# One more plain hidden pair, layer-1 modulation products on TensorE, and later sums in a two-layer diffusion block

## The chip, the cores and the metric

The kernel runs on one core of a Trainium2 chip. Its time is the device time of one execution in microseconds (us), and the number compared is the median over several runs. The profile is one further execution, recorded by the hardware.

## The reference

Two token streams pass two layers: 512 latent tokens and 256 context tokens, each 1024 wide. Layer 0 mixes with a gated linear recurrence and layer 1 with latent attention. After each mixer stands a gated feed-forward network with 2816 hidden units. Every norm is modulated by six vectors per layer that come from a condition `c` (latent) or `c_ctx` (context). Cut to what matters here:

```python
for i in range(DEPTH):                       # DEPTH = 2
    mod_lat = split(silu(c)    @ ada_w[i] + ada_b[i], 6)   # ada_w[i]: 1024 x 6144
    mod_ctx = split(silu(c_ctx) @ ada_w[i] + ada_b[i], 6)
    h = modulate(rmsnorm(x, norm_mix_g[i]), mod[0], mod[1])
    x = x + mod[2] * mixer_i(h)
    h = modulate(rmsnorm(x, norm_ffn_g[i]), mod[3], mod[4])
    x = x + mod[5] * ((silu(h @ Wg) * (h @ Wu)) @ Wout)    # 2816 hidden units = 22 tiles of 128
return rmsnorm(x, final_norm_g)
```

In layer 1 the context stream is needed by the attention alone (modulation vectors 0 and 1). The vectors 2 to 5 of layer 1 are used for latent tokens only.

## The kernel before, in words

Every large product is made from split operands: a float32 value is cut into a high and a low part (`wh`/`wl` for weights, `hh`/`hl` for normed tokens, `ah`/`al` for hidden activations), and three matmuls (high x high, low x high, high x low) stand for one. Tokens lie along the free dimension: latent 0 to 511, context 512 to 767.

**Weights.** `Stream` brings weights in: SyncE's queue loads up to 1 MB into one of two `raw` buffers, ScalarE makes `wh` (L108), VectorE (GpSimd in some stages) makes `wl` (L119). Four pairs of `wh`/`wl` units exist. `done(unit)` gives units back in order and lets `advance` split the next ones at this place of ScalarE's and VectorE's programs. Each engine works its own list in program order, and the program order is written by hand.

**Layer 0's feed-forward network** is `ffn0`. The 22 hidden tiles come in chunks of `PAIRS0 = (4, 2, 4, 4, 4, 4)`. After the hidden tiles of a chunk come eight output tiles (`out_tile`, m = 0 to 7), each added into `xT` by `residual` (L760) with a multiply-add on VectorE for latent and one for context tokens.
A hidden tile is a pair of products, gate and up. The first `PLAIN0` pairs are `plain`: two products of 48 matmuls each into two-bank PSUM tiles (`ps_main`, three of them). The others are `pair`: the gate and up blocks for two halves of the 768 tokens (A = 0 to 383, B = 384 to 767) are taken as a 2 x 2 block product made of seven products of 12 matmuls (in the order 1, 5, 6, 2, 7, 3, 4) into three one-bank PSUM tiles x, y, z. For these, `differences(kp)`, called four times, makes sums and differences of token blocks on VectorE and ScalarE (48 VectorE operations in all), and `sums` / `sum4` (L365 to L372) do the like for each weight tile.
Between plain pairs and seven-product pairs the PSUM layout changes from three two-bank tiles to six one-bank tiles. An output tile takes two banks. `split_hidden` cuts a hidden tile into `ah` and `al`; for a seven-product pair it is put off into the next pair, or to the end of the chunk. The first two output tiles of a chunk are begun with all but the last hidden tile.

**Layer-1 modulation.** `ada_w[1]` comes in 96 tiles of 128 x 512 (GpSimd's queue, 256 KB each, three buffers): six vectors `ch`, two halves each, eight row blocks `k` each. A call of `ada_step` is a *place* in the program; it takes one tile or `n` tiles. Each tile costs VectorE a multiply-add into `acc` (`ada_sum`, L535/L537), and for `ch` 0 and 1, needed for both streams, a second one for the other stream (L540/L542). When the eight tiles of a half are summed, the next call makes `ada_add`: small fp32 matmuls with a column of ones (`pick`, L558) sum over the 128 partitions into the PSUM tile `psada`. After the second half `ada_copy` (ScalarE, L565) takes it out, and some calls later `ada_evac` transposes it on TensorE (L519) and adds the bias. Layer 0's vectors 2 to 5 were made during the recurrence by another way: fp32 matmuls with `csil` (silu of both conditions, 32 columns wide) as stationary and the weight tile as moving operand, four column groups of 256 columns (L584).
By the code, 80 tiles of layer 1 (`ch` 0 to 4) are taken during `ffn0`: one at each plain pair, one in each `pair` (after product 2), one or two after each output tile. `ada_until(1, 4)` takes what is left behind the last hidden tile, ahead of the last eight output tiles. By the order of the calls six tiles are left there. The last 16 tiles (`ch` 5) are taken in `ffn(1, ...)`, three calls after each of the first hidden tiles.

Of the kernel before, what the change touches and what calls it, by code (L numbers as in the profile page):

```python
# [145 lines left out]
def kernel(ctx, tc, x, c, ctx_in, c_ctx, ada_w, ada_b, norm_mix_g, norm_ffn_g, ffn_w_in,  # L146
# [194 lines left out]
    PLAIN0 = 3  # L341
# [166 lines left out]
    def ada_evac(wait=False):  # L508
# [11 lines left out]
        pv = px[:, :256].rearrange("p (c j r) -> p j c r", c=2, j=4)  # L520
        for v in range(2):
            dve.tensor_tensor(mod[:, l, ch, v, :].rearrange("p (j c) -> p j c", j=4), pv[:, :, :, v],
                              adab(l, ch).rearrange("p (j c) -> p j c", j=4), op=ALU.add)
# [6 lines left out]
    def ada_sum(i, t, l, ch, k, half):  # L530


        both, first = ch < 2, acc[:, :512]
        if k == 0:
            dve.tensor_scalar(first, t, csil[:, k, int(both):int(both) + 1], None, op0=ALU.mult)  # L535
        else:
            dve.scalar_tensor_tensor(first, t, csil[:, k, int(both):int(both) + 1], first, op0=ALU.mult, op1=ALU.add)  # L537
        if both:
            if k == 0:
                dve.tensor_scalar(t, t, csil[:, k, 0:1], None, op0=ALU.mult)  # L540
            else:
                dve.scalar_tensor_tensor(t, t, csil[:, k, 0:1], ada_ps["lat"], op0=ALU.mult, op1=ALU.add)  # L542
            ada_ps["lat"] = t
        if k == KT - 1:
            ada_state["sums"] = (i, l, ch, half, [t, first] if both else [first])

    def ada_add():
        if ada_state["sums"] is None:
            return
        i, l, ch, half, sums = ada_state["sums"]  # L550
# [4 lines left out]
        for j in range(2):  # L555
            r = 64 * half + 32 * j
            for v, a in enumerate(sums):
                pe.matmul(ps[r:r + 32, :256], pick[:, v, :], a[:, j * 256:(j + 1) * 256],  # L558
                          start=v == 0, stop=v == len(sums) - 1)
# [7 lines left out]

    def ada_step(n=1):
        for _ in range(n):
            ada_evac(n == 1)  # L570
            ada_add()
            i = ada_state["used"]
            if i >= N_ADA[0]:
                return
            ada_fill()
            l, ch, k, *half = adas[i]
            t = ada_tiles.pop(i)
            if half:
                ada_sum(i, t, l, ch, k, *half)
            else:  # L580
                if k == 0:
                    ada_ps[0] = psa.tile([P, 512], F32, name=f"psada{i}", tag="ada")
# [1154 lines left out]
```

## Time and profile before

| what | value |
|---|---|
| median of 3 runs | 1620.7 us (1619.24 to 1623.19) |
| the profiled execution: its time / its span | 1622.39 / 1620.6 us |
| TensorE (PE) busy | 1516.2 us (94%) |
| VectorE (DVE) / ScalarE (ACT) / GpSimd (POOL) busy | 980.1 (60%) / 679.8 (42%) / 282.0 us (17%) |
| mean granted TensorE clock | 0.968 of full speed |

Busy time is the union of an engine's instructions, matmuls overlap one another in it. The granted clock is 1.00 at 2.4 GHz and 0.50 at 1.2 GHz; the value of a stretch is a mean over these two levels. A releaser (`<-`) names the instruction for which the engine waited. The stages around the change are: `ffn0`'s entry and plain pairs up to 427 us, its chunks to 898 us, the end of `ffn0` to 946 us, the attention to about 1225 us, and layer 1's feed-forward network from there.

### The profile page before, as it was taken

What the parts mean: (1) busy time and instruction counts of PE and PEld (TensorE: products, weight loads), DVE (VectorE), ACT (ScalarE), POOL (GpSimd) and SP (SyncE); (2) the same over time, 40 slices, a digit from 0 to 9 for tenths busy, and PEclk for the clock granted to TensorE, in tenths of its full rate; (3) what the DMA queues carried; (4) which work ended last, traced back from release to release, by engine and by line L of the source; (5) the groups of instructions that cost most, each with busy time, mean ns of one, the idle gap of its engine ahead of it and who ended that gap; (6) DMA issues with size and microseconds to landing.
All of it is one profiled execution on the core that took longest, in us unless ns stands there. A gap on an engine that the chain in (4) does not pass through costs nothing.

```text
span 1620.6 us, 21238 instructions
## 1 busy us (share of the span) xinstructions
PE 1516.2 (94%) x8667; PEld 1330.2 (82%) x8667; DVE 980.1 (60%) x1474; ACT 679.8 (42%) x998; POOL 282.0 (17%) x261
## 2 busy tenths in 40 slices
PE   7999989899799999999999799999999889999998
PEld 5887877688688998989889687899998668888887
DVE  5676777777877867767676466666537434323334
ACT  5476575543413331413314243666644222222223
POOL 3233333350000000011010243111144100000002
PEclk8999999999899999999999899999999999999999
DMA  9334343311233233243342222110112323233222
GB/s 359 113 118 127 107 130 93 103 58 41 73 97 104 85 98 98 82 146 105 105 143 86 65 59 69 28 41 27 53 53 92 137 85 104 79 104 114 79 80 91
DMA packets 137073, 155.11 MB, mean 96 GB/s; under 512 B 6283, under 2 KB 114432, under 8 KB 136976
## 3 DMA queue, kind: packets, MB, share of 16 engines
q1 hardware_dynamic: 124352, 112.21, 21.6%
q0 software_dynamic: 12320, 41.02, 8.2%
q8 instruction: 68, 1.11, 0.3%
q10 hardware_dynamic: 304, 0.53, 0.1%
q14 instruction: 29, 0.24, 0.0%
HBM read 151.64 MB, written 2.10 MB: 95 GB/s over the span
## 4 chain that ended last, share of the span: by engine, by line
PE 63%; issue 15%; DVE 15%; ACT 4%; DMA 1%; POOL 1%; SPq 0%; DVEq 0%; POOLq 0%; ACTq 0%
PE f L784 14%; PE fo L784 7%; PE fo L1206 6%; PE x L1160 4%; PE lo L784 3%; PE s L1536 3%; PE ga L784 2%; PE wo L784 2%; PE o L1578 2%; PE z L1160 2%; PE p L784 2%; PE g L784 2%; DVE yc L892 1%; PE t L1554 1%; PE y L1160 1%
## 5 line engine op out<-in xcount | busy, mean ns | idle before, releaser
L108 ACT ACTIVATE wh<-raw 128x1024 fp32r<-128x1024 f32 (+3 forms) x250 | 209.6, 865 | 215.7 <-PE fo L1206 63.5
L119 POOL TENSOR_TENSOR wl<-raw,wh 128x1024 fp32r<-128x1024 f32 (+3 forms) x66 | 158.1, 2406 | 327.2 <-ACT wh L108 321.5
L119 DVE TENSOR_TENSOR wl<-raw,wh 128x1024 fp32r<-128x1024 f32 (+2 forms) x184 | 170.4, 938 | 11.9 <-ACT wh L108 11.8
L760 DVE SCALAR_TENSOR_TENSOR xT<-fo,mod,xT 128x512 f32<-128x512 f32 (+1 forms) x124 | 74.3, 626 | 129.3 <-PE fo L1206 65.7
L239 POOL DMA_DIRECT2D ada<-in_ada_w_dram x96 | 51.7, 539 | 559.3 <-DVE ada L542 280.8
L784 PE MATMUL f<-hh,wh 128*128 128x512 f32 x320 | 126.1, 394 | 0.0
L784 PE MATMUL f<-hl,wh 128*128 128x512 f32 x320 | 125.5, 392 | 0.0
L784 PE MATMUL f<-hh,wl 128*128 128x512 f32 x320 | 125.3, 392 | 0.0
L778 POOL TENSOR_TENSOR acc<-acc,sq 128x256 f32<-128x256 f32 (+1 forms) x52 | 50.6, 973 | 335.4 <-ACT sq L776 334.2
L1206 PE MATMUL fo<-ah,wh 128*128 128x512 f32 (+1 forms) x352 | 100.2, 352 | 1.6 <-ACT ah L1194 1.6
L1101 DVE TENSOR_TENSOR sg<-sg,f 128x512 f32<-128x512 f32 x20 | 13.8, 688 | 142.1 <-ACT sg L1100 142.1
L1206 PE MATMUL fo<-al,wh 128*128 128x512 f32 (+1 forms) x352 | 98.6, 347 | 0.6 <-DVE al L1195 0.6
L1206 PE MATMUL fo<-ah,wl 128*128 128x512 f32 (+1 forms) x352 | 98.0, 345 | 0.0
L1100 ACT ACTIVATE sg<-f 128x512 f32<-128x512 f32 x20 | 12.0, 599 | 163.8 <-PE f L784 163.8
L784 PE MATMUL fo<-ah,wh 128*128 128x512 f32 (+1 forms) x200 | 72.9, 364 | 0.0
L784 PE MATMUL fo<-ah,wl 128*128 128x512 f32 (+1 forms) x200 | 72.7, 364 | 0.0
L784 PE MATMUL fo<-al,wh 128*128 128x512 f32 (+1 forms) x200 | 72.7, 364 | 0.0
L784 PEld LDWEIGHTS f<-hh,wh 128*128 128x128 f32 x320 | 60.8, 190 | 14.1 <-issue 1.6
L784 PEld LDWEIGHTS f<-hh,wl 128*128 128x128 f32 x320 | 60.6, 189 | 12.8
L784 PEld LDWEIGHTS f<-hl,wh 128*128 128x128 f32 x320 | 60.8, 190 | 12.6
L1206 PEld LDWEIGHTS fo<-ah,wh 128*128 128x128 f32 x352 | 59.4, 198 | 11.9 <-issue 2.9
L537 DVE SCALAR_TENSOR_TENSOR acc<-ada,csil,acc 128x512 f32<-128x512 f32 x84 | 62.8, 747 | 6.5 <-DMA ada<-in_ada_w_dram 5.6
(480 smaller groups left out, 4073.6 us busy)
## 6 DMA issues: line engine op xcount, KB each, us to landing
raw<-in_ffn_w_in_dram SPq DMA_DIRECT2D x24, 1024.0 KB, 4.9
ada<-in_ada_w_dram POOLq DMA_DIRECT2D x96, 256.0 KB, 3.1
raw<-in_ffn_w_in_dram SPq DMA_DIRECT2D x40, 512.0 KB, 4.8
raw<-in_ffn_w_out_dram SPq DMA_DIRECT2D x19, 1024.0 KB, 5.0
ada<-in_ada_w_dram POOLq DMA_DIRECT2D x30, 512.0 KB, 4.4
ada<-in_ada_w_dram SPq DMA_DIRECT2D x32, 256.0 KB, 5.5
raw<-in_lru_w_in_dram SPq DMA_DIRECT2D x10, 512.0 KB, 5.1
raw<-in_lru_gate_w_dram SPq DMA_DIRECT2D x16, 256.0 KB, 3.1
```

Of the source, the lines that this page charges most:

```text
L108: nc.scalar.activation(dst(hi), src(self.raw[load]), AF.Copy)
L119: self.low_engine.tensor_tensor(dst(lo), src(self.raw[load]), dst(hi).bitcast(F32), op=ALU.subtract)
L239: eng.dma_start(t, ada_w[l, k * P:(k + 1) * P, c0:c0 + 512])
L537: dve.scalar_tensor_tensor(first, t, csil[:, k, int(both):int(both) + 1], first, op0=ALU.mult, op1=ALU.add)
L760: dve.scalar_tensor_tensor(xT[:, m, s], ps(s) if callable(ps) else ps[:, s], mod[:, l, ch, v, m:m + 1], xT[:, m, s], op0=ALU.mult, op1=ALU ...
L778: accs.append(lambda: nc.gpsimd.tensor_tensor(acc[:, s], acc[:, s], sq, op=ALU.add))
L784: pe.matmul(ps[:, off + s.start:off + s.stop], a, b[:, s], start=first and i == 0, stop=last and i == 2)
L892: dve.scalar_tensor_tensor(y[:, s0:s1], ps[:, s0 + o:s1 + o], convw(tap, k), y[:, s0:s1], op0=ALU.mult, op1=ALU.add)
L1160: pe.matmul(ps, w[:, o:o + P], x[:, k0 + k, s], start=first and k == 0 and q == 0, stop=last and k == 3 and q == 2, skip_group_check=not f ...
L1206: pe.matmul(ps[v], w[:, o:o + P], x[:, k, s], start=k == 0 and q == 0, stop=k == nh - 1 and q == 2)
L1536: pe.matmul(ps[:, o:o + 384], x, y[:, k0:k1], start=j == 0, stop=j == 4)
L1578: pe.matmul(ps[:, :256], x[:, t % 4, hs], y[:, t, :], start=t == 0 and j == 0, stop=t == NT - 1 and j == 2)
```

## The change

- `PLAIN0` goes from 3 to 4: the whole first chunk is plain, and the first seven-product pair is that of hidden tile 4. `differences(1)` and later ones use another pool of temporaries, and the four `differences` are spread among the plain pairs in another order. The splits of plain pairs 2 and 3 and the copies of the late difference block go behind the last plain pair.
- `ada_product`: for `ch` 0 and 1 of layer 1 the 32 tiles are no longer summed on VectorE. Each is the moving operand of four fp32 matmuls of 128 columns in four column groups, with `csil` as the stationary operand, accumulated in `psada` over `k`.
- `ada_step`: with a finished half waiting, the first call does nothing, and only the second makes `ada_add`.
- In `pair` a call stands after product 1, and while `ch` 0 and 1 last a second one after product 2. In `ffn(1, ...)` there are two tiles between the gate and the up product and two behind the pair, in place of three behind it. After output tiles: one tile each while `ch` 0 and 1 last or in chunk 1, two later.
- Three output tiles are begun early in place of two (in the first chunk with two of four hidden tiles). The banks of a pair are taken as y, z, x. The last pair of a chunk is split at once, ahead of the release of its last weight unit.

```diff
     PAIRS0 = (4, 2, 4, 4, 4, 4)
-    PLAIN0 = 3
+    PLAIN0 = 4
...
     def ada_sum(i, t, l, ch, k, half):
...
+    def ada_product(i, t, l, ch, k, half=None):
+        n = 256 if half is None else 128
+        if k == 0 and not half:
+            ada_ps[0] = psa.tile([P, 512], F32, name=f"psada{i}", tag="ada")
+        o = (half or 0) * n
+        for j in range(4):
+            pe.matmul(ada_ps[0][32 * j:32 * j + 32, o:o + n], csil[:, k, :], t[:, j * n:(j + 1) * n],
+                      start=k == 0, stop=k == KT - 1)
+        if k == KT - 1 and half != 0:
+            ada_copy(i, l, ch, ada_ps[0])
+    def ada_one():
+        ada_fill()
+        i = ada_state["used"]
+        l, ch, *f = adas[i]
+        (ada_sum if l and ch > 1 else ada_product)(i, ada_tiles.pop(i), l, ch, *f)
+        ada_state["used"] += 1
+        ada_fill()
     def ada_step(n=1):
+        if ada_state["sums"]:
+            ada_state["calls"] += 1
+            if ada_state["calls"] < 2:
+                return
+            ada_add()
+        else:
+            ada_evac(True)
         for _ in range(n):
-            ada_evac(n == 1)
-            ada_add()
...
-            ada_fill()
+            if ada_state["used"] < N_ADA[0] and not ada_state["sums"]:
+                ada_one()
...
                     if pg is None:
                         pg, pu, off = pair_ps(f"f{l}{ph}{j}")
                         prod(pg, gu, hh, hl, sl)
+                        ada_step(2)
                         prod(pu, uu, hh, hl, sl, off=off)
                     elif pu is None:
                         pu, off = pg, SEQ
...
                     dve.tensor_tensor(al[:, j, :n], sg[:, :n], ah[:, j, :n].bitcast(F32), op=ALU.subtract)
                     st.done(gu)
                     st.done(uu)
-                    ada_step()
-                    ada_step()
-                    ada_step()
+                    ada_step(2)
                 if ph == 0:
                     ada_until(1, 5)
                 lastp = ph == len(ffn_units[l]) - 1
...
             def differences(kp):
-                if kp == 1:
+                if kp:
                     x = [[stemp(f"x{kp}{i}")[:, :H2] for i in range(2)], [ptemp(f"x{kp}{i}") for i in (2, 3)]]
                 else:
                     x = [tmp.tile([P, T], F32, name=f"x{kp}{i}", tag="nt") for i in range(2)]
...
                     st.done(s0_out[c][2][m // per])
             split = []
-            LATONLY = lambda: ada_state["used"] > 8 * KT
-            def pair(j, i):
+            on_pe = lambda: ada_state["used"] < 8 * KT
+            def pair(j, i, last):
                 g = tmp.tile([P, T], F32, name=f"g0{j}", tag="nt")
                 p5 = ptemp(f"p5{j}")
-                x, y, z = (ps_bank(f"{c}{j}")[:, :H2] for c in "xyz")
+                y, z, x = (ps_bank(f"{c}{j}")[:, :H2] for c in "yzx")
                 product(1, j, x, True, True)
                 act.activation(g[:, A], x, AF.Copy)
                 while split:
                     split.pop()()
                 release(1, j)
+                ada_step()
                 product(5, j, z, True, True)
                 act.activation(p5, z, AF.Copy)
                 release(5, j)
...
                 dve.tensor_tensor(g[:, A], g[:, A], y, op=ALU.add)
                 act.activation(g[:, A], g[:, A], AF.Silu)
                 release(2, j)
-                ada_step()
+                if on_pe():
+                    ada_step()
                 product(7, j, x, False, True)
                 dve.tensor_tensor(p5, p5, x, op=ALU.add)
                 release(7, j)
...
                 product(4, j, x, False, True)
                 dve.tensor_tensor(g[:, B], g[:, B], p5, op=ALU.mult)
                 dve.tensor_tensor(g[:, A], g[:, A], x, op=ALU.mult)
-                split.append(lambda: split_hidden(i, g))
+                if last:
+                    split_hidden(i, g)
+                else:
+                    split.append(lambda: split_hidden(i, g))
                 release(4, j)
             def plain(j, pg, pu):
...
                 if pu is None:
                     pu = ps_main(f"f0{j}u")
                     prod(pu, uu, hh, hl, SL)
-                if j == PLAIN0 - 1:
-                    act.activation(th[3], late[0].bitcast(F32), AF.Copy)
-                    dve.tensor_copy(tl[3], late[1].bitcast(F32))
                 g = tmp.tile([P, T], F32, name=f"g0{j}", tag="nt")
                 act.activation(g, pg[:, :T], AF.Silu)
                 dve.tensor_tensor(g, g, pu[:, :T], op=ALU.mult)
-                split_hidden(j, g)
+                if j < 2:
+                    split_hidden(j, g)
+                else:
+                    split.append(lambda: split_hidden(j, g))
                 st.done(gu)
                 st.done(uu)
-                ada_step()
             made = [ps_main(f"f0{j}g") for j in range(2)] + [ps_main("f00u")]
             entry([(s0_plain[0][0], made[0], 0, True), (s0_plain[1][0], made[1], 0, True),
...
             st.low_engine = dve
             plain(0, made[0], made[2])
             differences(0)
+            plain(1, made[1], None)
+            ada_step()
             differences(1)
-            plain(1, made[1], None)
+            plain(2, None, None)
+            ada_step()
             differences(2)
             differences(3)
-            for j in range(2, PLAIN0):
-                plain(j, None, None)
+            plain(3, None, None)
+            act.activation(th[3], late[0].bitcast(F32), AF.Copy)
+            dve.tensor_copy(tl[3], late[1].bitcast(F32))
+            ada_step()
+            while split:
+                split.pop(0)()
             ps_layout((6, 512))
             for c, (h0, nh, outs) in enumerate(s0_out):
                 for j in range(max(h0, PLAIN0), h0 + nh):
-                    pair(j, j - h0)
+                    pair(j, j - h0, j == h0 + nh - 1)
                 lastp = c == len(s0_out) - 1
-                while split:
-                    split.pop()()
                 if lastp:
                     ada_until(1, 4)
                     for m in range(KT):
...
                     boundary([lambda m=m: last(m) for m in range(KT)], nxt, at=(1, 2, 1))
                     return
-                two = [out_tile(c, m, (gb, ga), range(nh - 1)) for m in range(2)]
+                n0 = nh - 1 if c else 2
+                three = [out_tile(c, m, (gb, ga), range(n0)) for m in range(3)]
                 for m in range(KT):
-                    ps = out_tile(c, m, (gb, ga), (nh - 1,) if m < 2 else range(nh), two[m] if m < 2 else None)
+                    if m < 3:
+                        ps = out_tile(c, m, (gb, ga), range(n0, nh), three[m])
+                    else:
+                        ps = out_tile(c, m, (gb, ga), range(nh))
                     for g in (gb, ga):
                         residual(m, lambda s: ps[g[0]], 0, 5, g, False)
                     out_done(c, m)
-                    ada_step(1 if nh == 4 and not LATONLY() else 2 if nh == 4 else m % 2)
+                    ada_step(1 if nh < 4 or on_pe() else 2)
     na1 = Norm(1, 1, 0, CTXG, hh, hl, "m1a")
     nb1 = Norm(1, 1, 0, LATG, hh, hl, "m1b")
```

## Rows read from the trace of the kernel before

**Rows 1.** TensorE's waits from 387.2 to 908.9 us: in total, times, longest.
```profile
PE psada L558 <- DVE acc L537: 13.8, 3, 9.2
PE x L1160 <- DVE g L1265: 7.4, 1, 7.4
PE psada L558 <- DVE ada L542: 5.5, 3, 3.7
PE adax L519 <- ACT acc L565: 4.0, 3, 2.8
PE x L1160 <- DVE p L1240: 3.7, 4, 0.9
PE f02u L784 <- ACT wh L108: 2.9, 1, 2.9
PE f02u L784 <- DVE wl L119: 2.2, 1, 2.2
```
**Rows 2.** Stretches: length, PE, PEld, DVE, ACT, POOL busy, clock, DMA share, GB/s.
```profile
387.20:444.30 57.10, 44.61 (x230) 40.02 (x229) 48.66 (x82) 23.93 (x39) 1.61 (x3) 0.88 0.22 70
444.30:480.60 36.30, 34.76 (x202) 29.75 (x201) 26.68 (x42) 5.70 (x10) 3.77 (x7) 1.00 0.35 102
480.60:533.70 53.10, 49.77 (x275) 45.57 (x274) 40.01 (x65) 16.75 (x30) 3.23 (x6) 0.97 0.31 95
533.70:635.30 101.60, 96.00 (x540) 89.64 (x539) 71.81 (x114) 32.52 (x57) 6.46 (x12) 0.97 0.30 91
635.30:737.70 102.40, 97.83 (x550) 90.32 (x549) 71.99 (x117) 34.08 (x60) 10.76 (x20) 0.97 0.38 114
737.70:838.10 100.40, 95.68 (x541) 89.30 (x540) 67.25 (x110) 31.83 (x56) 10.76 (x20) 0.98 0.37 115
838.10:897.60 59.50, 59.35 (x341) 58.13 (x339) 42.02 (x67) 26.92 (x49) 3.23 (x6) 1.00 0.34 107
897.60:908.90 11.30, 1.57 (x8) 0.62 (x7) 7.07 (x9) 2.17 (x3) 1.61 (x3) 0.73 0.31 99
1253.10:1336.80 83.70, 70.99 (x300) 56.59 (x299) 31.39 (x39) 19.14 (x25) 5.64 (x11) 0.92 0.34 115
```
**Rows 3.** The chain that ended last, one seven-product product: start, length, matmuls.
```profile
434.02 2.08 PE x L1160 x12
```
**Rows 4.** Timeline of TensorE: output-tile matmuls, start and length, 512 + 256 columns.
```profile
464.36 0.51 PE L1206 MATMUL fo<-al,wh 128*128 128x512 f32 x2
464.71 0.51 PE L1206 MATMUL fo<-ah,wl 128*128 128x512 f32 x2
```
**Rows 5.** Timeline of TensorE around one and two modulation tiles during the recurrence.
```profile
60.55 0.51 PE L784 MATMUL p<-hh,wl 128*128 128x512 f32 x2
...
61.56 0.62 PE L784 MATMUL g<-hh,wh 128*128 128x512 f32 x2
...
88.13 0.51 PE L784 MATMUL g<-hh,wl 128*128 128x512 f32 x2
88.57 1.07 PE L584 MATMUL psada<-ada,csil 128*32 128x256 f32 x16
89.57 0.62 PE L784 MATMUL ga<-uh,wh 128*128 128x512 f32 x2
```
**Rows 6.** Timeline of TensorE around a sum with no wait before it.
```profile
875.75 0.34 PE L1160 MATMUL y<-hh,wl 128*128 128x384 f32 x1
...
876.57 0.45 PE L1160 MATMUL x<-t2h,wh 128*128 128x384 f32 x1
```
**Rows 7.** VectorE by groups: busy us, mean ns, idle before.
```profile
L1265 DVE TENSOR_TENSOR g<-g,f02u 128x768 f32<-128x768 f32 x1 | 1.0, 953 | 0.1
...
L537 DVE SCALAR_TENSOR_TENSOR acc<-ada,csil,acc 128x512 f32<-128x512 f32 x84 | 62.8, 747 | 6.5 <-DMA ada<-in_ada_w_dram 5.6
```
**Rows 8.** Loads of modulation tiles: size, median us from issue to landing.
```profile
ada<-in_ada_w_dram POOLq DMA_DIRECT2D x96, 256.0 KB, 3.1
```
**Rows 9.** TensorE's waits from 1253.1 to 1336.8 us (layer 1's feed-forward network).
```profile
PE psada L558 <- DVE acc L537: 12.7, 2, 6.6
```

More of the change, by code (lines that the diff above doesn't have):

```diff
@@ L530, in ada_sum @@
     def ada_sum(i, t, l, ch, k, half):
-        both, first = ch < 2, acc[:, :512]
+        total, col = acc[:, :512], csil[:, k, 0:1]
         if k == 0:
-            dve.tensor_scalar(first, t, csil[:, k, int(both):int(both) + 1], None, op0=ALU.mult)
+            dve.tensor_scalar(total, t, col, None, op0=ALU.mult)
         else:
[L537 to L543, printed above, removed]
+            dve.scalar_tensor_tensor(total, t, col, total, op0=ALU.mult, op1=ALU.add)
         if k == KT - 1:
-            ada_state["sums"] = (i, l, ch, half, [t, first] if both else [first])
+            ada_state["sums"], ada_state["calls"] = (i, l, ch, half, total), 0
     def ada_add():
@@ L549, in ada_add @@
             return
-        i, l, ch, half, sums = ada_state["sums"]
+        i, l, ch, half, total = ada_state["sums"]
         ada_state["sums"] = None
@@ L556, in ada_add @@
             r = 64 * half + 32 * j
-            for v, a in enumerate(sums):
-                pe.matmul(ps[r:r + 32, :256], pick[:, v, :], a[:, j * 256:(j + 1) * 256],
-                          start=v == 0, stop=v == len(sums) - 1)
+            pe.matmul(ps[r:r + 32, :256], pick[:, 0, :], total[:, j * 256:(j + 1) * 256], start=True, stop=True)
         if half == 1:
@@ L566, in ada_copy @@
         ada_state["evac"], ada_state["calls"] = (i, l, ch, sb), 0
-    def ada_step(n=1):
-        for _ in range(n):
-            ada_evac(n == 1)
-            ada_add()
-            i = ada_state["used"]
-            if i >= N_ADA[0]:
-                return
-            ada_fill()
[L576 to L582, printed above, removed]
-                for j in range(4):
-                    pe.matmul(ada_ps[0][32 * j:32 * j + 32, :256], csil[:, k, :], t[:, j * 256:(j + 1) * 256],
-                              start=k == 0, stop=k == KT - 1)
-                if k == KT - 1:
-                    ada_copy(i, l, ch, ada_ps[0])
-            ada_state["used"] += 1
-            ada_fill()
+    def ada_product(i, t, l, ch, k, half=None):
[15 more added lines that the diff above has]
+        ada_fill()
+    def ada_step(n=1):
+        if ada_state["sums"]:
[5 more added lines that the diff above has]
+            ada_evac(True)
+        for _ in range(n):
+            if ada_state["used"] < N_ADA[0] and not ada_state["sums"]:
+                ada_one()
     def ada_until(l, ch):
         n = sum(1 for a in adas if a[:2] <= (l, ch)) - ada_state["used"]
-        if n > 0:
-            ada_step(n)
+        for _ in range(n):
+            ada_add()
+            ada_evac()
+            ada_one()
         if n >= 0:
```

8 lines of the change are left out of this document (5 added, 3 removed).

## The prediction, on record before the changed kernel ran

> **What bounds the kernel now.** I read the waits of TensorE first, then its busy time by stretch, then single matmuls. TensorE does nearly all of the work in a row. In the last four pairs of `ffn0` it is busy 59.35 of 59.50 us [rows 2]. So a stretch has a floor, its matmuls back to back, and the question is how far above it the stretch lies. The reader is to see three kinds of excess. First, idle time with a name: between 387 and 909 us TensorE waits 13.8 + 5.5 us for modulation sums (`psada` on `acc` and `ada`), 4.0 us for a modulation copy, 7.4 us at the first seven-product pair and 2.9 + 2.2 us for the weights of plain pair 2 [rows 1]. Another 12.7 us goes to sums in layer 1's feed-forward network [rows 9]. Second, a lower clock behind such waits: the stretches that hold them show a granted clock of 0.88 to 0.98, those without show 1.00 [rows 2], so part of these matmuls ran at 1.2 GHz and not 2.4 GHz. Third, the sums' own matmuls. VectorE is not the bound by its total (48.66 of 57.10 us at the most [rows 2]), but it works in order, and TensorE stands still where it asks for the last sum too early.
>
> **Unit prices.** A product of a seven-product pair is 2.08 us [rows 3], a pair 7 x 2.08 = 14.6. A matmul of 512 and one of 256 columns take 0.35 us together [rows 4]. A plain product is 24 of these, 8.4 us, so a plain pair is 16.8. An output tile of four hidden tiles is 12 of them, 4.2 us, eight tiles 33.6. One one-row sum costs TensorE 876.57 - 875.75 - 0.17 (a matmul's own step, 2.08 / 12) = 0.65 us [rows 6].
>
> **Modulation tiles on TensorE.** The nearest rows are layer 0's, with 256 columns in four groups. One tile between two products costs 61.56 - 60.55 - 0.35 = 0.66 us; two tiles cost 89.57 - 88.13 - 0.35 = 1.09 [rows 5]. The second adds 0.43, so 0.23 is paid once per interruption. The new tiles have 128 columns, an estimated 0.22 + 0.23 = 0.445 us each, 32 of them 14.2 us. The bounds are 32 x 0.215 = 6.9 (nothing for the interruption) and 32 x 0.66 = 21.1. I take the middle because each tile stands alone between products, as in the first row.
> The Trainium skill (TensorEngine Tiling (Array Packing), Key Properties) says that a change of the tiling mode, not only of the tile, drains TensorE. This speaks against the change, which spreads 32 interruptions over the stage; by it the 6.9 of the low bound is out of reach, and the 0.23 us of the rows agree.
> What goes in return: the four two-row sums of `ch` 0 and 1, 0.65 + 0.43 = 1.08 us each, 4.3 in all, and 64 VectorE operations of 0.75 us at most [rows 7], 48 us that lie beside TensorE's work. The loads stay (80 of 256 KB on GpSimd's queue), but 32 of their buffers are now freed by TensorE. A tile lands 3.1 us after its issue [rows 8] and three are in flight; at two places TensorE passes three of them in 3 x (1.04 + 0.445) = 4.5 us, so I put this new wait at nothing, at most 2 us a chunk. If it came, every matmul would be queued behind it.
>
> **Stretch by stretch [rows 2].** Each line is what I expect against the length before.
> Plain pairs, 57.10 us. After: the products f01u, f02g, f02u, f03g, f03u, 5 x 8.4 = 42.0; three modulation tiles 1.3; then the first output tile must wait until VectorE has read f03u out of PSUM, 0.95 [rows 7] plus some 0.3. Sum 44.6, gain 12.5. The fourth plain pair costs 16.8 for 14.6, and this is in the sum. VectorE's share: the four `differences` (48 operations of about 0.5) are 24 us, products, splits and weights of the plain pairs about 14, together 38 of 43 us, and `plain(1)` now stands behind one `differences`, not two, which brings f02u's weights by about 6 us forward: 5.1 us of waits go. The 7.4 us wait was VectorE's backlog ahead of its last read; in the new order the backlog ends about 2 us before f03u does. What is late next is the split of tiles 2 and 3 (copies, two `ah`, two `al`, some 6 us); three early output tiles of two hidden tiles cover 6.2. Bounds: 8 to 12.8.
> First output tiles, 36.30: 33.6 + 8 x 0.445 = 37.2. Loss 0.9 (up to 3, if the split is late).
> Chunk 1, 53.10: 14 x 2.08 + 16.8 + 12 x 0.445 + 0.3 for a transpose = 51.5. Gain 1.6 (0 to 2.5). The wait for its last hidden tile (part of the 3.3 us in which TensorE is idle there [rows 2]) is covered by three early tiles of 1.04 us in place of two, and the split stands ahead of the weights of `release`.
> Chunk 2, 101.60: 58.2 + 33.6 + 9 x 0.445 + 0.65 + 0.3, and 1 us that I leave for waits, = 97.8. Gain 3.8 (2 to 5).
> Chunks 3 and 4, 102.40 and 100.40: each 58.2 + 33.6 + two sums 1.3 + 0.3 + 1 = 94.4. Gains 8.0 and 6.0 (4 to 9, 3 to 7).
> Last pairs, 59.50: 58.2. Gain 1.3; the waits on `p` (0.9 each [rows 1]) go, as VectorE's sum stands after product 1.
> `ada_until`, 11.30: before, six tiles are left there. Counting the new calls place by place (3 at plain pairs, 8, 4 + 8, 8 + 8 with one tile each, then the sums) I find none left: only one sum (0.65), `ada_copy` behind ScalarE's split and weights, and a transpose. I put it at 4.0. Gain 7.3 (5 to 9).
> Layer 1's feed-forward network, 83.70: six hidden tiles of 48 matmuls of 512 columns, 0.173 x 512 / 384 = 0.23 each [rows 3], are 66.2 (a tile 11.0); with two sums, a transpose and 0.5 us left 68.3. Gain 15.4 (12 to 16.5), the two waits of 12.7 [rows 9] and the low clock behind them. The call that does nothing gives VectorE 11 us more for the last sum.
> Early tiles, bank order and the moved split add no instruction; their cover is the work on hidden tiles already split (three output tiles of 3.1 us in a chunk of four). Without it TensorE would wait for one split, about 2 us a chunk.
> Sum: 12.5 - 0.9 + 1.6 + 3.8 + 8.0 + 6.0 + 1.3 + 7.3 + 15.4 = 55.0. The profiled execution took 1622.4 us (span 1620.6, 1.8 about it), so 1567.4; the median of the runs lies 1.7 below it, so I say **1566 us**. By the low bounds (8 - 3 + 0 + 2 + 4 + 3 + 0.5 + 5 + 12 = 31.5) it is 1589. The high bounds with the cheapest modulation tiles (7.3 less) give 1551.
>
> **Rivals.**
> *The waits come back as bank waits.* Three early tiles hold all six PSUM banks, and their residuals come within 3 us; VectorE then also has two sums a place and the next weights. By my count it is 6 to 8 us late at the fourth residual. Past 8.3 us (two output tiles) TensorE waits for banks, and the late sum waits again. For it: VectorE busy 72 of 102.4 us in chunk 3 [rows 2], and that work comes in less time. Against it: no wait for `xT` among the rows [rows 1]. If chunks 2 to 4 gain only their pairs' part, about 16 us of the gain is lost: 1582.
> *The weights set the pace (slower).* In `ffn0` two `raw` buffers feed ScalarE's and VectorE's splits. If these run at their limit, each wait taken away returns as a wait on `wh` or `wl`, and TensorE's added work remains: 2.2 for the plain pair + 14.2 - 4.3 = 12.1 us, so 1633. The sum's gain of 55.0 is 67.1 gross less this 12.1; the time is slower than before once more than 55 of the 67 us come back so. Against it: the only weight waits are 5.1 us at f02u [rows 1], and the pairs run at 59.35 of 59.50 with DMA at 0.34 [rows 2].
> *The waits were hidden by something else and nothing changes*: within 5 us of 1621.
> *Better than the sum*: no leftover waits, tiles at the low bound: 1551.
>
> **Numbers.** Forecast 64% (its own range 1555 to 1580), bank waits 18% (1575 to 1600), weights 6%, no change 3%, better 9%. The range 1552 to 1592 leaves out the slower and unchanged cases and the tails of two others, about 2 in 10. Faster by over 0.3% (about what a measurement here can tell): 0.91, within 0.3%: 0.03, slower: 0.06.
>
> **What would show it.** TensorE's waits on `psada` under 4 us in all; no wait longer than 3 us at f02u or at the first seven-product pair; the first output tile some 45 us after plain pair 0's products; 4 us between the last pair and the last output tiles; six hidden tiles of layer 1 in 68 us; an interruption by a modulation tile of 0.45 us. I would be wrong if waits for `xT` or `wl` appear in the output phases, if modulation tiles wait for their loads, or if interruptions cost 1 us.

## The result, and the profile after

The changed kernel takes 1571.4 us (median of four runs, 1565.7 to 1573.0), the kernel before 1621.95 in the same comparison. The ratio is 0.9684, with a 95% interval of 0.9656 to 0.9713: 51 us or 3.2% faster. The forecast was 1566 us, its range 1552 to 1592. The profiled execution took 1571.8 us (span 1569.9). Line numbers moved: the output tiles are now L1212, a plain product L791, a seven-product one L1166, the pick sums L554, the modulation products L570, ScalarE's copy of them L560, VectorE's sums L538/L540; in the kernels of the experiments some of them move again.

First the stretches of the profile after, in the form and order of [rows 2]: plain pairs, first output tiles, chunks 1 to 4, last pairs, what lies before the last output tiles, and six hidden tiles of layer 1.

```profile
389.90:434.40 44.50, 43.74 (x265) 36.96 (x264) 35.20 (x60) 19.43 (x30) 1.51 (x3) 1.00 0.18 60
434.40:472.70 38.30, 38.30 (x256) 30.61 (x256) 19.99 (x30) 6.92 (x11) 3.87 (x8) 1.00 0.38 111
472.70:526.70 54.00, 53.51 (x367) 45.79 (x363) 32.46 (x55) 16.73 (x31) 6.46 (x12) 1.00 0.39 117
526.70:624.70 98.00, 98.00 (x610) 89.27 (x607) 62.06 (x102) 32.56 (x58) 10.54 (x20) 1.00 0.38 114
624.70:718.30 93.60, 93.60 (x541) 88.19 (x540) 66.02 (x106) 32.76 (x58) 8.82 (x17) 1.00 0.38 117
718.30:811.80 93.50, 93.50 (x541) 88.07 (x540) 66.01 (x106) 32.74 (x58) 8.61 (x16) 1.00 0.35 113
811.80:870.10 58.30, 58.30 (x338) 58.06 (x336) 42.42 (x67) 26.83 (x48) 1.61 (x3) 1.00 0.30 93
870.10:873.10 3.00, 0.82 (x7) 0.33 (x7) 1.97 (x3) 2.06 (x3) 0.00 (x0) 1.00 0.38 115
1218.60:1285.60 67.00, 67.00 (x298) 54.24 (x298) 31.89 (x38) 19.16 (x25) 5.92 (x11) 1.00 0.42 144
```

TensorE is busy all the time in six of the nine, and the granted clock is 1.00 in each, where before it was 0.73 to 1.00 [rows 2]. The waits of TensorE from 389.9 to 873.2 us (in total, times, longest) are these three, in place of the list of [rows 1]:

```profile
PE adax L519 <- ACT acc L560: 2.2, 1, 2.2
PE fo L1212 <- DVE g L1273: 0.8, 1, 0.8
PE fo L1212 <- DVE al L1201: 0.4, 1, 0.4
```

Layer 1's six hidden tiles show no wait at all (12.7 us in [rows 9]). Stretch by stretch:

| stretch | before | forecast | after |
|---|---|---|---|
| plain pairs | 57.1 | 44.6 | 44.5 |
| first output tiles | 36.3 | 37.2 | 38.3 |
| chunk 1 | 53.1 | 51.5 | 54.0 |
| chunk 2 | 101.6 | 97.8 | 98.0 |
| chunk 3 | 102.4 | 94.4 | 93.6 |
| chunk 4 | 100.4 | 94.4 | 93.5 |
| last pairs | 59.5 | 58.2 | 58.3 |
| before the last output tiles | 11.3 | 4.0 | 3.0 |
| six hidden tiles, layer 1 | 83.7 | 68.3 | 67.0 |
| sum of gains | | 55.0 | 55.2 |

The span fell by 50.7 only, since code that the change doesn't touch was longer in this execution: the plain pairs began 2.8 us later (389.9 for 387.1), and the attention with layer 1's entry took some 3 us more (309.8 for 306.8), while the last output tiles were 1.9 us shorter (35.7 for 37.6). Over all twelve profiles of this study the beginning lies between 386.5 and 391.1 us, and the attention with layer 1's entry takes 305.4 to 309.9 us. So stretches of `ffn0` and layer 1's network are compared below, beside the times.

### The profile page after: what moved, and what is told of

It is laid out like the page before. It is cut to its first block, busy times and chain, and to the rows that moved or that the text cites. A ratio compares the mean times of both kernels' runs of the same rounds, so it can differ in the third digit from the quotient of the medians.

```text
span 1569.9 us, 21629 instructions
## 1 busy us (share of the span) xinstructions
PE 1512.2 (96%) x8903; PEld 1321.4 (84%) x8903; DVE 934.2 (60%) x1397; ACT 675.9 (43%) x989; POOL 281.5 (18%) x261
## 4 chain that ended last, share of the span: by engine, by line
PE 82%; DVE 11%; ACT 4%; issue 1%; DMA 1%; SPq 0%; POOL 0%; DVEq 0%; ACTq 0%; POOLq 0%
PE f L791 14%; PE fo L1212 11%; PE x L1166 10%; PE fo L791 8%; PE z L1166 5%; PE lo L791 3%; PE s L1555 3%; PE ga L791 2%; PE wo L791 2%; PE y L1166 2%; PE o L1597 2%; PE p L791 2%; PE g L791 2%; DVE yc L899 1%; PE t L1573 1%
## 5 line engine op out<-in xcount | busy, mean ns | idle before, releaser
L767 DVE SCALAR_TENSOR_TENSOR xT<-fo,mod,xT 128x512 f32<-128x512 f32 (+1 forms) x124 | 74.1, 626 | 129.8 <-PE fo L1212 66.2
L791 PE MATMUL f<-hh,wh 128*128 128x512 f32 x320 | 124.7, 390 | 0.0
L791 PE MATMUL f<-hh,wl 128*128 128x512 f32 x320 | 124.5, 389 | 0.0
L791 PE MATMUL f<-hl,wh 128*128 128x512 f32 x320 | 124.5, 389 | 0.0
L785 POOL TENSOR_TENSOR acc<-acc,sq 128x256 f32<-128x256 f32 (+1 forms) x52 | 50.7, 975 | 374.1 <-ACT sq L783 371.9
L1212 PE MATMUL fo<-ah,wh 128*128 128x512 f32 (+1 forms) x352 | 98.3, 345 | 0.9 <-DVE g L1273 0.8
L1212 PE MATMUL fo<-al,wh 128*128 128x512 f32 (+1 forms) x352 | 95.8, 338 | 0.4 <-DVE al L1201 0.4
L1212 PE MATMUL fo<-ah,wl 128*128 128x512 f32 (+1 forms) x352 | 95.3, 337 | 0.0
L791 PE MATMUL fo<-ah,wh 128*128 128x512 f32 (+1 forms) x200 | 73.0, 365 | 0.0
L791 PE MATMUL fo<-ah,wl 128*128 128x512 f32 (+1 forms) x200 | 72.7, 364 | 0.0
L791 PE MATMUL fo<-al,wh 128*128 128x512 f32 (+1 forms) x200 | 72.7, 364 | 0.0
L791 PEld LDWEIGHTS f<-hh,wh 128*128 128x128 f32 x320 | 60.1, 188 | 13.2 <-issue 0.8
L791 PEld LDWEIGHTS f<-hh,wl 128*128 128x128 f32 x320 | 60.1, 188 | 12.6
L791 PEld LDWEIGHTS f<-hl,wh 128*128 128x128 f32 x320 | 60.1, 188 | 12.4
L1212 PEld LDWEIGHTS fo<-ah,wh 128*128 128x128 f32 x352 | 56.2, 188 | 12.8 <-issue 4.6
L1212 PEld LDWEIGHTS fo<-al,wh 128*128 128x128 f32 x352 | 56.2, 188 | 8.0 <-DVE al L1201 0.7
```

What stands on the lines that cost most here:

```text
L767: dve.scalar_tensor_tensor(xT[:, m, s], ps(s) if callable(ps) else ps[:, s], mod[:, l, ch, v, m:m + 1], xT[:, m, s], op0=ALU.mult, op1=ALU ...
L785: accs.append(lambda: nc.gpsimd.tensor_tensor(acc[:, s], acc[:, s], sq, op=ALU.add))
L791: pe.matmul(ps[:, off + s.start:off + s.stop], a, b[:, s], start=first and i == 0, stop=last and i == 2)
L1212: pe.matmul(ps[v], w[:, o:o + P], x[:, k, s], start=k == 0 and q == 0, stop=k == nh - 1 and q == 2)
```

## The experiments

The theory: the gain is TensorE's named waits and the low clock behind them, and each part of the change removes its own. The rivals: one part does most of it, or the parts only move waits. Each kernel is the changed one with the edit shown (`...` stands for lines left out); medians are of four runs, ratios against the kernel before in the same comparison.

**Three plain pairs, the old order.** The temporaries of `differences` (the `if kp` line) go back with it.
```diff
-    PLAIN0 = 4
+    PLAIN0 = 3
...
-                if kp:
+                if kp == 1:
...
-            plain(1, made[1], None)
-            ada_step()
             differences(1)
-            plain(2, None, None)
+            plain(1, made[1], None)
...
-            plain(3, None, None)
+            plain(2, None, None)
```


> The changed kernel with three plain pairs again and the old order of plain pairs and differences; everything else stays changed. Theory (the fourth plain pair and its order are worth 12.6 us): from plain pair 1's up product to the first output tile the stretch is 54 to 57 us (44.5 in the changed kernel), with TensorE's waits at plain pair 2's weights (4 to 5 us) and at the first seven-product pair (6 to 8 us) back; all other stretches as in the changed kernel; about 1583 us. Rival (the modulation sums on VectorE made that backlog): the waits stay under 4 us together, the stretch is 48 us or less, about 1575 us.


1580.2 us, ratio 0.9757 (0.9738 to 0.9777). Plain pairs and the first seven-product pair take 54.9 us, where four plain pairs take 44.5. Three waits of 8.4 us are back, and the clock of the stretch is 0.91:
```profile
PE x L1166 <- DVE g L1273: 4.5, 1, 4.5
PE f02u L791 <- DVE wl L119: 2.3, 1, 2.3
PE f02u L791 <- ACT wh L108: 1.6, 1, 1.6
```
In the kernel before they were 12.5 us [rows 1]; the 4 us that did not come back go with the rest of the change, by which part of it no run shows.

**Three plain pairs, the new order** of `differences`.
```diff
-    PLAIN0 = 4
+    PLAIN0 = 3
...
-                if kp:
+                if kp < 0:
...
-            plain(2, None, None)
-            ada_step()
             differences(2)
             differences(3)
-            plain(3, None, None)
+            plain(2, None, None)
```


> The changed kernel with three plain pairs, but plain pair 1 ahead of the second call of differences, as in the changed kernel. Theory (VectorE's 24 us of differences have to end before the first seven-product pair, and only the fourth plain pair covers them): the wait at plain pair 2's weights goes, and the wait at the first seven-product pair grows to 10 to 13 us; stretch 54 to 57 us, about 1583 us, as with the old order. Rival (the order alone does it): no wait over 4 us, stretch about 47 us, about 1575 us.


1578.7 us, 0.9749 (0.9733 to 0.9766). The waits for the weights of pair 2 are gone, and all of it stands in one place:
```profile
PE x L1166 <- DVE g L1273: 11.9, 1, 11.9
```
The stretch is 56.1 us. The new order without the fourth plain pair only moves VectorE's backlog; the pair is what covers it. Of the 12.6 us that the stretch gained, 10 to 12 (10.4 and 11.6) come with that pair. Whether four plain pairs would need the new order was not run.

**Sums at the next place**, as before.
```diff
             ada_state["calls"] += 1
-            if ada_state["calls"] < 2:
-                return
             ada_add()
```


> The changed kernel, but a finished half is summed at the very next place. Theory (TensorE waited because it asked for the sum one place too early): waits on psada return, 1 to 4 us each at the sums between output tiles of chunks 2 to 4 (3 to 4 of them), with a lower clock behind the longer ones, and 0 to 2 us in layer 1's feed-forward network, where two tiles a place halve the haste; 6 to 14 us slower than the changed kernel, 1577 to 1585 us. Rival (VectorE's relief and the other places did it): under 1 us of waits on psada, 1570 to 1573 us.


1586.15 us, 0.9797 (0.9776 to 0.9817), the slowest of the ten. The output phases of chunks 2 to 4 take 39.6, 42.4 and 40.4 us (35.0, 35.3, 35.2 after), layer 1's six tiles 69.8 (67.0). The clock of the three output phases is 0.96, 0.92 and 0.96. The wait for the sums, in `ffn0`:
```profile
PE psada L554 <- DVE acc L540: 12.5, 4, 5.9
```
The longest, on VectorE's timeline (start, length, idle before):
```profile
700.08 0.69 DVE L365 TENSOR_TENSOR s<-raw 128x512 f32<-128x512 f32 x1
700.80 0.69 DVE L366 TENSOR_TENSOR raw<-raw 128x512 f32<-128x512 f32 x1
...
704.33 1.14 DVE L765 SCALAR_TENSOR_TENSOR xT<-fo,mod,xT 128x512 f32<-128x512 f32 x2
705.38 0.74 DVE L540 SCALAR_TENSOR_TENSOR acc<-ada,csil,acc 128x512 f32<-128x512 f32 x1
707.03 0.75 DVE L540 SCALAR_TENSOR_TENSOR acc<-ada,csil,acc 128x512 f32<-128x512 f32 x1 [0.91 <-DMA ada<-in_ada_w_dram]
```
and on TensorE's:
```profile
707.93 1.07 PE L554 MATMUL psada<-acc,pick 128*32 128x256 f32 x4 [5.90 <-DVE acc L540]
```
The last multiply-add stands behind weight sums, residuals and its own load. In the kernel after, the same sum is asked for at 713.40 us, and VectorE's last multiply-add for it ended at 710.8:
```profile
710.03 0.75 DVE L540 SCALAR_TENSOR_TENSOR acc<-ada,csil,acc 128x512 f32<-128x512 f32 x1 [0.54 <-DMA ada<-in_ada_w_dram]
```
It was ready 2.6 us early. One output tile (4.2 us) before, at about 709.2, it was not. The two lines of code are worth 15 us of the time, the largest single part (19 us by the stretches: 16.6 in `ffn0` and 2.8 in layer 1's tiles).

**Modulation sums of `ch` 0 and 1 on VectorE again**, everything else as after.
```diff
-        (ada_sum if l and ch > 1 else ada_product)(i, ada_tiles.pop(i), l, ch, *f)
+        (ada_sum if l else ada_product)(i, ada_tiles.pop(i), l, ch, *f)
...
-                ada_step()
+                ada_step(1 if j < 18 else 2)
...
-                    ada_step(1 if nh < 4 or on_pe() else 2)
+                    ada_step(1 if c < 2 else 2)
```
(with the two-row sums of the kernel before, and two tiles a place from chunk 2 on, so that none is left over).


> The changed kernel with the modulation tiles of vectors 0 and 1 of layer 1 summed on VectorE for both kinds of tokens (two operations a tile, two-row sums), taken a place later; two tiles a place from chunk 2 on and in the last pairs, so that none is left. Theory A (being late is enough; the products on TensorE only cost): 32 interruptions of 0.56 us go and four two-row sums of 1.1 us come, 13 us less on TensorE, 1557 to 1560 us. Theory B (VectorE must be relieved): its 48 us come back as waits of TensorE on p, on xT and on psada and as a later first output tile, 10 to 25 us in all, 1568 to 1585 us.


1578.66 us, 0.9743 (0.9726 to 0.9761). Without the tiles on TensorE the first output tiles and chunk 1 are 6.9 us shorter (34.6 + 50.8 for 38.3 + 54.0), and the plain pairs 0.8. Chunk 2 is 10 us longer, with VectorE busy 79.87 of 108.00 us and a clock of 0.97; the stretches of chunks 1 and 2, columns as above:
```profile
466.50:517.30 50.80, 48.30 (x276) 44.39 (x275) 44.05 (x70) 16.54 (x30) 4.84 (x9) 1.00 0.35 107
517.30:625.30 108.00, 98.12 (x548) 90.75 (x547) 79.87 (x131) 32.90 (x58) 12.27 (x23) 0.97 0.37 112
```
and TensorE's waits from the plain pairs to the last output tiles:
```profile
PE psada L562 <- DVE ada L546: 6.6, 2, 5.5
PE x L1175 <- DVE p L1257: 5.3, 3, 3.4
PE psada L562 <- DVE acc L541: 5.2, 2, 2.6
```
The products cost TensorE 17.9 - 4.3 = 13.6 us (below), and without them these 17.1 us of waits stand, with matmuls at a lower clock behind some; the difference is 7 us of the time, 11 by the stretches of `ffn0`. But not all of it is VectorE's relief. At the end of chunk 2, where the last tile of `ch` 1 is done, this kernel is only 2.3 us behind the changed one (237.1 us from the start of the plain pairs, for 234.8). The other 9 us come later: chunk 3 takes 97.6 us (93.6) and chunk 4 96.2 (93.5), where VectorE has the same one-row sums in both kernels (busy 66.2 us in chunk 3, 66.0 after), only at other places, and 5.2 of the 17.1 us of waits (the row with `acc`) stand there. So the products pay for themselves, but by some 2 us; the rest is where the later sums fall. All sums on VectorE with places that suit them were not run.

**Two early output tiles, old banks, old split.**
```diff
-                y, z, x = (ps_bank(f"{c}{j}")[:, :H2] for c in "yzx")
+                x, y, z = (ps_bank(f"{c}{j}")[:, :H2] for c in "xyz")
...
-                three = [out_tile(c, m, (gb, ga), range(n0)) for m in range(3)]
+                three = [out_tile(c, m, (gb, ga), range(n0)) for m in range(2)]
```
(and the last pair's split put off to the end of the chunk again).


> The changed kernel with two early output tiles, the banks taken as x, y, z and a chunk's last hidden tile split behind the release of its weights, as before the change. Theory (these edits only cover the split): the wait for the last hidden tile in chunk 1 comes back (0.4 us now, 2 us then), and in the first chunk the output tiles wait 0 to 2 us for hidden tiles 2 and 3; chunks 2 to 4 and the rest as in the changed kernel within 0.5 us a stretch; 1571 to 1576 us. Rival (three early tiles and the bank order cost as much as they save, as residuals bunch): chunks 2 to 4 get shorter by 0.5 us or more each, 1567 to 1571 us.


1569.8 us, 0.9664 (0.9646 to 0.9682), no different from the kernel after. Chunk 1's output tiles take 23.7 us for 22.4, with waits of 1.2 us for `ah` and 0.6 for `al`; the last pairs with the sum behind them are 0.7 us shorter, and no other stretch moves by more than 0.1. In chunks 2 to 4 two early tiles cover the split as three do. The three edits together are worth about 1 us by the stretches; the times don't show it.

**Two products at every second place.**
```diff
     def ada_step(n=1):
...
             ada_evac(True)
+        i = ada_state["used"]
+        if 4 * KT <= i < 8 * KT:
+            ada_state["skip"] = not ada_state.get("skip", False)
+            if ada_state["skip"]:
+                return
+            n = 2
         for _ in range(n):
```
(the added lines stand behind the `if`/`else`).


> The changed kernel with the 32 modulation tiles on TensorE taken two at every second place: the same matmuls in 16 interruptions. Theory (an interruption costs 0.34 us beyond its matmuls, 0.56 in all): each double one costs 0.78 us, 16 x 0.34 = 5.4 us less, first output tiles 36.5 to 37 us in place of 38.3, about 1566 us. Rival (a second tile is not there in time, with three in flight): waits on the loads at TensorE, up to 1 us at each double place, no gain or a loss, 1570 to 1580 us.


1563.9 us, 0.9634 (0.9611 to 0.9657). Plain pairs to chunk 2 take 44.4 + 37.1 + 52.9 + 96.5 us: 3.9 shorter than after. One interruption by two tiles, on TensorE's timeline:
```profile
470.80 0.34 PE L1172 MATMUL x<-hh,wl 128*128 128x384 f32 x1
471.06 0.65 PE L570 MATMUL psada<-ada,csil 128*32 128x128 f32 x16
471.64 0.44 PE L1172 MATMUL z<-t0h,wh 128*128 128x384 f32 x1
471.92 0.34 PE L1172 MATMUL z<-t0l,wh 128*128 128x384 f32 x1
```
and one by a single tile, in the kernel after:
```profile
474.72 0.34 PE L1166 MATMUL x<-hh,wl 128*128 128x384 f32 x1
474.99 0.42 PE L570 MATMUL psada<-ada,csil 128*32 128x128 f32 x8
475.35 0.45 PE L1166 MATMUL z<-t0h,wh 128*128 128x384 f32 x1
475.63 0.34 PE L1166 MATMUL z<-t0l,wh 128*128 128x384 f32 x1
```
From the matmul before to the second matmul after it is 471.92 - 470.80 = 1.12 us with two tiles and 475.63 - 474.72 = 0.91 with one; two steps of 0.17 are the product's own. A single tile thus costs 0.57 us, and the second adds 0.21: 0.36 is paid once per interruption. Sixteen interruptions fewer should give 16 x 0.36 = 5.8, and the stretches gave 3.9. Two of the sixteen lie in the plain pairs, which didn't get shorter (44.4 us for 44.5), and a wait for a load took 0.7:
```profile
PE psada L570 <- DMA ada<-in_ada_w_dram: 0.7, 1, 0.7
```
The last 0.5 us is not accounted for.

**One vector on VectorE, one on TensorE.**
```diff
-        (ada_sum if l and ch > 1 else ada_product)(i, ada_tiles.pop(i), l, ch, *f)
+        (ada_sum if l and ch != 1 else ada_product)(i, ada_tiles.pop(i), l, ch, *f)
...
-                ada_step()
+                ada_step(1 if on_pe() else 2)
...
-                    ada_step(1 if nh < 4 or on_pe() else 2)
+                    ada_step(1 if c < 2 or on_pe() else 2)
```


> The changed kernel with vector 0 of layer 1 summed on VectorE for both kinds of tokens (the first 16 tiles, in the plain pairs and chunks 0 and 1, where VectorE had time in the run with all sums on VectorE) and vector 1 still on TensorE; two tiles a place in the later pairs. Theory (VectorE's room, not its total, decides): the first output tiles and chunk 1 take some 6 us less than in the changed kernel, chunk 2 keeps its 98 us within 1 us, no wait on psada over 1 us; 1565 to 1567 us. Rival (any sum for both kinds on VectorE brings waits): over 3 us of waits on psada, p or xT, 1570 us or more.


1577.35 us, 0.971 (0.9687 to 0.9733). The first output tiles are 34.6 us as hoped, but chunk 1's take 27.7 (22.4), and chunk 4's pairs, now with two tiles a place, 64.3 (58.3), with a wait of 3.4 us for `p` among them. The theory fell, by its handovers. The first product of `ch` 1 waited 3.30 us for ScalarE's copy of `ch` 0 out of the PSUM tile:
```profile
514.82 0.66 PE L579 MATMUL psada<-ada,csil 128*32 128x128 f32 x8 [3.30 <-ACT acc L569]
```
and on ScalarE that copy stood behind a weight split which waited for VectorE:
```profile
513.87 0.63 ACT L108 ACTIVATE wh<-raw 128x512 fp32r<-128x512 f32 x1 [4.03 <-DVE raw L372]
514.40 0.37 ACT L569 ACTIVATE acc<-psada 128x256 f32<-128x256 f32 x1
```

**The same with later sums.** The places in the pairs take one tile again, as in the kernel after. `ch` 0's last sum comes two places later still, `ch` 1's tiles go in twos among chunk 2's pairs, and the last sum of all inside the last pair:
```diff
-            if ada_state["calls"] < 2:
+            both, half = ada_state["sums"][2] == 0, ada_state["sums"][3]
+            if ada_state["calls"] < (4 if both and half else 2):
                 return
             ada_add()
+            if both and half:
+                return
...
+        if 6 * KT <= ada_state["used"] < 8 * KT:
+            if ada_state["used"] == 6 * KT and not ada_state.get("skip"):
+                ada_state["skip"] = True
+                return
+            n = 2
...
+                if j == 21:
+                    ada_add()
```


> Vector 0 of layer 1 summed on VectorE as in the run with one vector each, but its last sum is taken two places later and no product stands in that place; vector 1 on TensorE two tiles a place, all in chunk 2's pairs but the first two; the last sum of the stage taken inside the last pair. Theory (the loss of the run with one vector each was the haste at the change-over, not VectorE's load): first output tiles 34.6 us, chunk 1 52 us or less, chunk 2 96 us or less, last pairs with sum 59.5, 10 to 12 us less than the changed kernel, 1559 to 1562 us. Rival (VectorE is full there): over 3 us of waits on p, psada or xT in chunks 1 and 2, 1566 us or more.


1562.6 us, 0.9637 (0.9621 to 0.9652). The waits of 3.3 and 3.4 us of the last kernel are gone, and none is over 1.1. The first output tiles and chunk 1 are 35.2 + 50.2 us, 6.9 less than after, but chunk 2, which now holds all of `ch` 1, is 99.8 (98.0; 96 or less was expected). It ends no better than the simpler kernels around it. Nor is it worse: half of the modulation tiles are back on VectorE here, and the time is that of the kernels with two products at a place, 1563.9 above and 1563.1 below. With its sum asked for late enough, `ch` 0 did not need TensorE.

**Two products, and the last sum inside the last pair** (the edit of the experiment "Two products at every second place", and `ada_add()` after product 7 of pair 21).


> The run with two products at every second place, with the last modulation sum of the stage taken inside the last seven-product pair. Theory (the wait of 2.2 us behind the last pair is ScalarE's copy, asked for too late): the last pairs with the sum take 59 to 59.6 us in place of 61.4, all else equal, 1561 to 1563 us. Rival (ScalarE's copy is late because of its splits): the wait stays above 1 us, 61 us.


1563.1 us, 0.9646 (0.9624 to 0.9667). Last pairs and sum take 59.2 us, 2.2 less than after. The eight output tiles behind them then take 37.0 (35.7), with waits for the split of the last hidden tile, which the 2.2 us ahead of them had covered:
```profile
PE fo L1218 <- DVE al L1207: 0.6, 1, 0.6
PE fo L1218 <- ACT ah L1206: 0.2, 1, 0.2
```
Net 1 us, which the times don't resolve.

**Layer 1: three calls behind each hidden tile**, as before, with the late sum.
```diff
-                        ada_step(2)
...
-                    ada_step(2)
+                    ada_step()
+                    ada_step()
+                    ada_step()
```


> The changed kernel with three one-tile calls behind each hidden tile of layer 1's feed-forward network, as before the change, with sums still one call late. Theory (a late call helps only if TensorE has work between the calls; three calls in a row have none): waits on psada of 3 to 6 us return at one or both sums, six hidden tiles in 72 to 82 us in place of 67.0, 1576 to 1586 us. Rival (one call later is enough by itself): 67 to 68 us, 1571 us.


1567.2 us, 0.9668 (0.9651 to 0.9685), no different from the kernel after. Layer 1's six tiles are 67.0 us as after, with no wait. The theory that the spread matters fell. The call that does nothing pushes the sum behind the next hidden tile; VectorE's last multiply-adds on its timeline:
```profile
1231.17 1.53 DVE L540 SCALAR_TENSOR_TENSOR acc<-ada,csil,acc 128x512 f32<-128x512 f32 x2
```
and the sum on TensorE's:
```profile
1236.98 0.62 PE L554 MATMUL psada<-acc,pick 128*32 128x256 f32 x4
```
It is ready 4.3 us before it is asked for. With the spread and without the delay (third experiment) 2.6 us of waits stay. Either does nearly all, the delay alone does all.

## Why the prediction was right, point by point

**Waits and clock.** Confirmed. Each named wait of [rows 1] and [rows 9] that the sum counted is gone, and the clock is 1.00 in the nine stretches. Going back to three plain pairs, to sums at the next place or to sums on VectorE brings waits of 8 to 17 us back; the spread of the calls in layer 1 alone brings none. One reading was too broad: the first output tiles of the kernel before hold a wait too (TensorE busy 34.76 of 36.30 us), and their clock is 1.00 all the same [rows 2].

**Plain pairs.** 44.5 for 44.6. VectorE's backlog ended at 431.1 us, 2.3 before it could read f03u, as was worked out (about 2); the wait of 0.8 us for that read is the one forecast (0.95 and some overhead). The first two experiments show that the fourth pair is the cover, and that the order without it is not.

**The modulation tiles: the mis-sized term.** The count was right (32 tiles: 3, 8, 12 and 9 by stretch), the price was 0.445 us and is 0.56 (0.57 among the products, worked out above; 0.55 in an output tile, by the starts 457.53 and 458.78 us below, less two steps of 0.35). The chosen 0.22 + 0.23 was read from the matmul before a tile to the first one after it; it left out that this first one steps 0.28 us and not 0.17. In all that is 32 x 0.56 = 17.9 us and not 14.2, inside the bounds of 6.9 to 21.1. It is most of the 1.1 and 2.5 us by which the first output tiles and chunk 1 are longer than forecast; chunk 1 also has a wait of 0.4 for its last hidden tile's split, and about 0.6 us there is not accounted for. TensorE's timeline in an output tile:
```profile
457.53 0.51 PE L1212 MATMUL fo<-ah,wl 128*128 128x512 f32 x2
457.97 0.43 PE L570 MATMUL psada<-ada,csil 128*32 128x128 f32 x8
458.33 0.62 PE L1212 MATMUL fo<-ah,wh 128*128 128x512 f32 x2
458.78 0.40 PE L1212 MATMUL fo<-al,wh 128*128 128x512 f32 x1
```
The Trainium skill (TensorEngine Tiling (Array Packing), Key Properties) says that a change of tiling mode drains TensorE. The trace agrees as far as it goes: 0.36 us is paid per interruption beyond the tile's own matmuls, and 16 interruptions fewer made the stretches 3.9 us shorter; that a drain is the reason, no run here shows. By that rule two tiles at a time are the better form, and they were.

**Late sums.** Chunks 3 and 4 are 0.8 and 0.9 us better than forecast: the 1 us left for waits in each was not needed. Layer 1's tiles are 67.0 for 68.3: 0.5 us was left for waits there, and the matmuls' step is 0.226 us (14 steps from 1218.64 to 1221.81) and not 0.23, 1.0 us less over 288 of them.

**Before the last output tiles.** 3.0 for 4.0: no tile left, and of the 3.0 us 2.2 are the copy by ScalarE behind its split, as described.

**Early tiles.** Costed at nothing, as cover for a split; they are worth 1 us in chunk 1. The 2 us a chunk that TensorE would wait without any cover were not tested, as no kernel went below two early tiles.

**The rivals.** Bank waits: none for `xT` in `ffn0`'s output phases, and 93.5 of 93.5 us busy in chunk 4. The lateness of VectorE stayed under the 8.3 us from which this rival decides; how far was not measured. Weights as the pace: no wait for `wh` or `wl` with four plain pairs; it is real only with three in the old order (3.9 us). Loads of modulation tiles: none, and 0.7 us once two tiles are taken at a place.

**The sum.** 55.0 forecast and 55.2 measured, with the errors of single stretches (-2.5 to +1.3) cancelling; that they cancel so well is luck. The median is 5 us above 1566. In the profiled execution, 0.4 us from the median, this is the lengths of the unchanged code told above. How the parts share the gain can't be read as a sum of the experiments: by time, late sums 15, fourth plain pair 7 to 9, products on TensorE 7, early tiles 0; together some 30 of 51. By the stretches of `ffn0` and layer 1's tiles the same four are 19, 11 to 12, 11 (of which 2 up to the end of chunk 2) and 1, together some 43 of 55. Of the rest, the 16.7 us of layer 1's tiles go by the delay or by the spread, either alone giving 13.9 or more, so that no kernel which undoes one of them shows it; and the added places, which leave no tile ahead of the last output tiles (8.3 us), were not undone by themselves.

A better version than the change came out: two products at a place, 1563 to 1564 us. About 4 us of the 7.5 are shown in the stretches; in the profiled executions the rest lies in the unchanged code, and the intervals of the two ratios just touch.

## What to carry to other kernels

Where an in-order engine needs another engine's partial result, ask for it a place later before moving any work: two lines were worth 15 us here, more than the moved products, of which half turned out not to be needed. Work that interrupts a stream of large matmuls is best priced from the matmul before it to the second matmul after it, and done in few, larger portions. When VectorE has a backlog at a change of stage, a cruder form of the work on TensorE (16.8 us for 14.6) can be cheaper than the cleverer one that must wait. And a kernel that differs by one part also moves everything behind it to other places: read what the part is worth from the stretch in which it stands, and not from the time alone.

## What was not expected of the hardware

The beginning of the plain pairs goes with how two instructions meet during the recurrence, in code that is the same in all kernels. In the profile before, VectorE's multiply takes 0.96 us, in the profile after 3.60; GpSimd's weight subtract begins 0.47 and 0.40 us behind it. VectorE before:
```profile
266.29 0.96 DVE L957 TENSOR_TENSOR tg<-tg,tg 128x768 f32<-128x768 f32 x1
```
GpSimd before:
```profile
266.76 2.73 POOL L119 TENSOR_TENSOR wl<-raw,wh 128x1024 fp32r<-128x1024 f32 x1
```
VectorE after:
```profile
265.46 3.60 DVE L964 TENSOR_TENSOR tg<-tg,tg 128x768 f32<-128x768 f32 x1
```
GpSimd after:
```profile
265.86 2.38 POOL L119 TENSOR_TENSOR wl<-raw,wh 128x1024 fp32r<-128x1024 f32 x1
```
Where VectorE takes 3.60 us, it ends 0.8 us behind GpSimd's subtract, which takes 2.38; where VectorE takes 0.96, the subtract takes 2.73. TensorE's wait behind it is 5.1 us in the one case and 2.3 in the other. Of the twelve profiles four show 5.1 (after and the three experiments from "One vector on VectorE" to "last sum inside the last pair"; GpSimd begins 0.38 to 0.40 us behind) and eight 2.3 (0.47 or 0.48 us behind). So 2.8 us of any comparison of single executions here lie in code that no edit touches. Each kernel has one profile, so whether one kernel goes both ways is not shown. The Trainium skill (SBUF — State Buffer, SBUF: two separate sides) says that VectorE, with two SBUF inputs, and GpSimd take one pair of ports as a whole, and that the one that starts first holds it for its instruction. The trace agrees that VectorE can be held up for the length of GpSimd's instruction (0.96 us becomes 3.60 beside a subtract of 2.38); by the recorded starts it is VectorE that starts first in both cases and loses in one, so these starts don't say who holds the ports.
